# Two recurrence units get their first four k tiles in the opening, and one attention unit moves between the pairs

## The chip, the cores and the metric

The kernel runs on one core of one Trainium2 chip. The metric is the device time of one execution in microseconds. Before the change three runs took 2498.23 to 2498.86 us, median 2498.66.

## The reference, cut to what matters

A stream x of 256 tokens and 2048 features goes through two layers, each a mixer and a SwiGLU feed-forward network. Every sublayer starts with an RMS norm and a modulation by a vector c (shift, scale and gate are products of silu(c) with a large matrix, mod_w). The first mixer is the one that the change touches:

```python
def hgrn2_fox_mixer(h, w_in, w_out, lower_bound, a_out_gain, q_gain, k_gain, f_bias):
    proj = h @ w_in
    qa, fa, ia, ga, qb, kb, vb, gb, fb = jnp.split(proj, cuts, axis=-1)
    ...
    forget = lb + (1 - lb) * sig
    o_a = chunk_gated_linear_recurrence(jax.nn.silu(split_heads(qa, A_HEADS)), key,
                                        split_heads(ia, A_HEADS), log_forget)
    o_a = merge_heads(rms_norm(o_a, ...)) * jax.nn.silu(ga)
    q = rms_norm(split_heads(qb, B_HEADS), q_gain)
    ...
    o_b = forgetting_attention(q, k, split_heads(vb, B_HEADS), log_f)
    o_b = merge_heads(o_b) * jax.nn.sigmoid(gb)
    return jnp.concatenate([o_a, o_b], axis=-1) @ w_out
```

Eight recurrence heads (HGRN2) and eight attention heads (FoX), all 128 wide, share one input projection.

## The kernel before, in words

**Units.** Two heads make a unit: A0 to A3 for the recurrence, B0 to B3 for attention. A unit needs two products of 512 output columns: for A the half 0 gives forget gate and value, half 1 query and output gate; for B half 0 gives query and key, half 1 value and gate. A20 is half 0 of A2, and so on.

**Products.** k runs over 16 tiles of 128 features. Weights are float32 and are split into a rounded part hi (a cast on ScalarE, L167) and the rest lo (a subtraction on VectorE, L169); each k tile and each half of the tokens takes three matmuls, hi with hi, lo with hi, hi with lo (L190 to L192, 128x512). One piece is two k tiles: 12 matmuls. Raw weights come in tiles of 1 MiB (four k tiles of 512 columns), through three buffers "raw"; hi and lo have four buffers each. A product's sum lies in PSUM, 128x2x512, two buffers "pp" (tag "acc" in the trace).

**The opening** (start(), up to about 148 us) is written out by hand: on every engine the order is the program's. Weights of A00, A01, A10 and A11 lie together in start_w, 1 MiB for each k tile. For every k tile SyncE (SP) fetches two 1 MiB rows of mod_w (mod_s, L984) and one tile of start_w (raw_s, L989); VectorE sums the two mod rows with silu(c) (mod_sum, L109), which gives shift and scale for the 128 features; ScalarE forms the modulated operand (tm_s, L1015, hT_s, L1016); TensorE multiplies it with the four column groups, each with two token halves: 24 split matmuls for a group of four (L1031 to L1033: 4 x 2 x 3), or in six "plain" steps (k tiles 0, 3, 6, 9, 12, 15) eight float32 matmuls without a split (L1026; the trace counts 16 instructions). Mod rows alternate between two buffers "modraw" and the pool "h" (eight buffers). SP issues in program order, and a transfer that waits for its buffer holds up everything behind it. Within the first tile, x is normed and transposed on TensorE in four blocks.

**After the opening** the pieces follow a list: A20, A21, A30, A31, then B00 to B31, then the output projection O0. A scheduler sets the order of instructions on each engine, from the order in which drive() writes them. Ahead of each piece drive() takes steps from a list of jobs, by due time: each job has a number of ticks (pieces) in which to be done (table TICKS): the recurrence of a unit (hgrn: qkT, exponents L459, exp L460, decay products L487, scores L515, state picks L548, output L555 to L558, norm L650), the attention's probabilities and outputs, and the forget line of all attention heads (fox_gates). When half 0 of a unit ends, the job of the unit two before is finished by force. At the end of a B half 1 the value is copied out of PSUM and the gate g_B is formed in four steps, the last reader of that PSUM buffer being L794 on VectorE. Rows of mod_w for later sublayers are summed along the way.

In the tags "qk", "kd", "dec" and "st" a job's tiles have one or two buffers, so a unit's tiles wait for an older unit's.

## Time and profile before

| | |
|---|---|
| median of three runs | 2498.66 us |
| profiled execution, its own time | 2495.23 us |
| its span | 2493.5 us |
| TensorE busy, VectorE busy, ScalarE busy | 2442.0, 1772.8, 1168.8 us |
| granted TensorE clock, mean | 0.997 |
| opening: last plain matmul group ends | 147.5 us |
| A20 begins, B00 begins, O0 begins | about 148.7, 267, 496 us |

The profile is of one execution. "PE" is TensorE, "DVE" VectorE, "ACT" ScalarE, "SPq" SyncE's queue. A row of a group of instructions gives line, engine, operation, what it writes and reads, how many, busy time, mean duration in ns, and after the bar the idle time of the engine just before them with what ended it. TensorE's matmuls overlap: the duration of one is longer than the distance of two starts.

### The profile page before, as it was taken

How to read it: one execution, taken by the hardware profiler on the slowest of the kernel's cores; microseconds unless marked ns; L12 is line 12 of the kernel's file. 1: busy time of each engine (PE TensorE's matmuls, PEld its weight loads, DVE VectorE, ACT ScalarE, POOL GpSimd, SP SyncE). 2: the span in 40 equal slices, each digit the busy share in tenths (PEclk: the TensorE clock that was granted, in tenths of full speed). 3: DMA queues.
4: the chain of work that ended last, by engine and by line, in shares of the span. 5: the costliest groups of instructions: out<-in, count | busy, mean ns of one | idle time of the engine just before them, and what ended most of it. 6: DMA issues, size and time to landing. Idle time of an engine off the chain costs nothing.

```text
span 2493.5 us, 28661 instructions
## 1 busy us (share of the span) xinstructions
PE 2442.0 (98%) x11204; PEld 2002.5 (80%) x11204; DVE 1772.8 (71%) x2039; ACT 1168.8 (47%) x1625; POOL 89.6 (4%) x176
## 2 busy tenths in 40 slices
PE   7899999999999999999999999999999999999999
PEld 4578887887888888888888888888888888888887
DVE  6967887887788767767767787876776554644555
ACT  4255555545434444344345666654544344344343
POOL 0000000000000000000000000000000000000000
PEclk9999999999999999999999999999999999999999
DMA  9964767985798877777786667677486555555554
GB/s 390 420 258 168 286 253 290 347 320 215 288 367 339 318 285 285 289 286 283 286 292 208 236 246 248 250 280 260 175 313 237 188 195 189 188 191 193 190 189 148
DMA packets 93849, 647.48 MB, mean 260 GB/s; under 512 B 10417, under 2 KB 10993, under 8 KB 16401
## 3 DMA queue, kind: packets, MB, share of 16 engines
q1 hardware_dynamic: 70290, 476.59, 52.4%
q0 software_dynamic: 23424, 169.07, 18.2%
q8 instruction: 87, 1.43, 0.2%
q14 instruction: 48, 0.39, 0.0%
HBM read 641.39 MB, written 4.23 MB: 259 GB/s over the span
## 4 chain that ended last, share of the span: by engine, by line
PE 93%; DVE 4%; DMA 2%; ACT 1%; issue 1%; SPq 0%; ACTq 0%
PE acc_F L192 13%; PE acc_F L190 13%; PE acc_F L191 13%; PE acc_G L190 6%; PE acc_G L192 6%; PE acc_G L191 6%; PE acc_C L192 4%; PE acc_C L190 4%; PE acc_C L191 4%; PE acc_B L190 2%; PE acc_B L192 2%; PE acc_B L191 2%; PE acc_O L190 2%; PE acc_O L192 2%; PE acc_O L191 2%; DMA raw_s<-in_start_w_dram 2%
## 5 line engine op out<-in xcount | busy, mean ns | idle before, releaser
L169 DVE TENSOR_TENSOR lo<-raw_F,hi 128x1024 fp32r<-128x1024 f32 x352 | 429.5, 1223 | 302.3 <-ACT hi L167 302.1
L167 ACT CAST hi<-raw_F 128x1024 fp32r<-128x1024 f32 x352 | 370.6, 1054 | 478.1 <-PE acc_F L192 433.2
L192 PE MATMUL acc_F<-hi,hT_f 128*128 128x512 f32 x1408 | 551.1, 391 | 1.4 <-DVE hT_f L357 1.4
L190 PE MATMUL acc_F<-hi,hT_f 128*128 128x512 f32 x1408 | 548.7, 390 | 1.8 <-ACT hT_f L356 1.8
L191 PE MATMUL acc_F<-lo,hT_f 128*128 128x512 f32 x1408 | 548.4, 390 | 0.0
L109 DVE SCALAR_TENSOR_TENSOR mod<-mod,silu_c 128x2048 f32<-128x2048 f32 x160 | 365.3, 2284 | 4.2 <-DMA mod<-in_mod_w_dram 4.2
L169 DVE TENSOR_TENSOR lo<-raw_G,hi 128x1024 fp32r<-128x1024 f32 x176 | 214.2, 1222 | 139.3 <-ACT hi L167 139.1
L167 ACT CAST hi<-raw_G 128x1024 fp32r<-128x1024 f32 x176 | 185.4, 1055 | 268.5 <-PE acc_G L192 227.3
L192 PEld LDWEIGHTS acc_F<-hi,hT_f 128*128 128x128 f32 x1408 | 264.4, 188 | 56.9 <-DVE hT_f L357 3.0
L190 PEld LDWEIGHTS acc_F<-hi,hT_f 128*128 128x128 f32 x1408 | 264.5, 188 | 55.8 <-ACT hT_f L356 2.2
L191 PEld LDWEIGHTS acc_F<-lo,hT_f 128*128 128x128 f32 x1408 | 264.3, 188 | 55.1
L190 PE MATMUL acc_G<-hi,ct_f 128*128 128x512 f32 x704 | 273.5, 389 | 1.6 <-DVE res_G L405 1.6
L192 PE MATMUL acc_G<-hi,ct_f 128*128 128x512 f32 x704 | 274.4, 390 | 0.0
L191 PE MATMUL acc_G<-lo,ct_f 128*128 128x512 f32 x704 | 273.7, 389 | 0.0
L190 PEld LDWEIGHTS acc_G<-hi,ct_f 128*128 128x128 f32 x704 | 132.2, 188 | 29.6 <-DVE res_G L405 2.4
L191 PEld LDWEIGHTS acc_G<-lo,ct_f 128*128 128x128 f32 x704 | 132.2, 188 | 27.4
L192 PEld LDWEIGHTS acc_G<-hi,ct_f 128*128 128x128 f32 x704 | 132.2, 188 | 27.2
L190 PE MATMUL acc_C<-hi,hT_n 128*128 128x512 f32 x384 | 152.4, 399 | 0.9 <-ACT hT_n L356 0.9
L192 PE MATMUL acc_C<-hi,hT_n 128*128 128x512 f32 x384 | 151.3, 394 | 0.7 <-DVE hT_n L357 0.7
L191 PE MATMUL acc_C<-lo,hT_n 128*128 128x512 f32 x384 | 151.7, 395 | 0.0
L104 POOL DMA_DIRECT2D mod<-in_mod_w_dram x160 | 84.5, 528 | 1612.8 <-DVE mod L109 1449.8
L169 DVE TENSOR_TENSOR lo<-raw_C,hi 128x1024 fp32r<-128x1024 f32 x96 | 116.1, 1220 | 35.2 <-ACT hi L167 34.8
(343 smaller groups left out, 3399.7 us busy)
## 6 DMA issues: line engine op xcount, KB each, us to landing
raw_F<-in_ffn_w_in_dram SPq DMA_DIRECT2D x176, 1024.0 KB, 4.9
mod<-in_mod_w_dram POOLq DMA_DIRECT2D x160, 1024.0 KB, 5.2
raw_G<-in_ffn_w_out_dram SPq DMA_DIRECT2D x88, 1024.0 KB, 4.9
raw_C<-in_gla_w_in_dram SPq DMA_DIRECT2D x48, 1024.0 KB, 5.6
mod_s<-in_mod_w_dram SPq DMA_DIRECT2D x32, 1024.0 KB, 17.0
raw_B<-in_ab_w_in_dram SPq DMA_DIRECT2D x32, 1024.0 KB, 6.6
raw_s<-in_start_w_dram SPq DMA_DIRECT2D x16, 1024.0 KB, 13.9
raw_A<-in_ab_w_in_dram SPq DMA_DIRECT2D x16, 1024.0 KB, 5.0
```

The lines of the kernel that those rows point to most:

```text
L104: nc.gpsimd.dma_start(out=tile, in_=a["mod_w"][l, part * KT + j])
L109: nc.vector.scalar_tensor_tensor(tile, tile, 1.0, silu_c, ALU.mult, ALU.mult, accum_out=modc[l, part][:, j:j + 1])
L167: nc.scalar.copy(out=hi, in_=w)
L169: env["lo"] = nc.vector.tensor_tensor(lo, w, hi, ALU.subtract)
L190: nc.tensor.matmul(o, a_hi, w_hi, start=(kt == 0), stop=False)
L191: nc.tensor.matmul(o, a_hi, w_lo, start=False, stop=False)
L192: nc.tensor.matmul(o, a_lo, w_hi, start=False, stop=(kt == last))
```

## The change

Four more steps, e0 to e3, come first in the opening. They multiply k tiles 0 to 3 with the four column groups of A2 and A3 (a new array early_w, 1 MiB for each k tile). Their sums are copied from PSUM into two tiles of the pool "h" by eight copies on ScalarE, and PSUM is then used for A0 and A1's steps s0 to s15. A20, A21, A30 and A31 later begin at k tile 4 (piece 2 of 8), and an addition on VectorE brings in the stored sum when a product ends. The plain steps are now e0, s5, s8, s11 and s15. Of the mod rows part 0 always goes to "modraw" and part 1 to "h". Weights, sums and operand of the second step move to between two blocks of the transposition of x. The table for silu is loaded after step e3's copies. The units are ordered A0, A1, B0, A2, A3, B1, B2, B3, TICKS of the first two recurrences go from 12 and 19 to 8 and 16, and the unit whose job is finished by force is the one two before in the new order.

Line numbers after the change are larger by 3 (up to the middle of the program) to 36.

SP's queue in the opening, from the mod rows of tile 2 on; mod_s_k are mod rows of k tile k, raw_s the weights of A0 and A1. Before:

```order
L984 DMA mod_s_2_267<-in_mod_w_dram 128x2048
L984 DMA mod_s_2_269<-in_mod_w_dram 128x2048
L984 DMA mod_s_3_271<-in_mod_w_dram 128x2048
L984 DMA mod_s_3_273<-in_mod_w_dram 128x2048
L989 DMA raw_s_275<-in_start_w_dram 128x2048
L984 DMA mod_s_4_317<-in_mod_w_dram 128x2048
L984 DMA mod_s_4_319<-in_mod_w_dram 128x2048
L989 DMA raw_s_321<-in_start_w_dram 128x2048
L984 DMA mod_s_5_363<-in_mod_w_dram 128x2048
L984 DMA mod_s_5_365<-in_mod_w_dram 128x2048
```

After (raw_se are the early weights, raw_ss those of A0 and A1):

```order
L987 DMA mod_s_3_271<-in_mod_w_dram 128x2048
L987 DMA mod_s_3_273<-in_mod_w_dram 128x2048
L993 DMA raw_se_275<-in_early_w_dram 128x2048
L993 DMA raw_se_317<-in_early_w_dram 128x2048
L993 DMA raw_ss_359<-in_start_w_dram 128x2048
L993 DMA raw_ss_409<-in_start_w_dram 128x2048
L993 DMA raw_ss_444<-in_start_w_dram 128x2048
L987 DMA mod_s_4_478<-in_mod_w_dram 128x2048
L987 DMA mod_s_4_480<-in_mod_w_dram 128x2048
L993 DMA raw_ss_482<-in_start_w_dram 128x2048
L987 DMA mod_s_5_516<-in_mod_w_dram 128x2048
L987 DMA mod_s_5_518<-in_mod_w_dram 128x2048
```

Five weight tiles now stand in a row ahead of the mod rows of k tile 4.

ScalarE in the opening after the change, from the end of e3's operand to the first cast of s1 (hi_s from raw_se and raw_ss are the casts of weights; "waits" names the engine or queue whose signal is waited for):

```order
L170 CAST hi_s_0_361<-raw_se_317 128x1024 [waits DMAHW1_49,PE_49]
L170 CAST hi_s_1_365<-raw_se_317 128x1024 [waits PE_49]
L1137 COPY early_393<-acc_e_129 128x512 [waits PE_49]
L1137 COPY early_393<-acc_e_129 128x512
L1137 COPY early_394<-acc_e_130 128x512 [waits PE_49]
L1137 COPY early_394<-acc_e_130 128x512
L1137 COPY early_393<-acc_e_0_263 128x512 [waits PE_49]
L1137 COPY early_393<-acc_e_1_264 128x512 [waits PE_49]
L1137 COPY early_394<-acc_e_0_265 128x512 [waits PE_49]
L1137 COPY early_394<-acc_e_1_266 128x512 [waits PE_49]
L1124 ACT_TABLE_LOAD
L170 CAST hi_s_0_412<-raw_ss_359 128x1024 [waits DMAHW2_49,DVE_49]
```

The casts of s0 stand behind the eight copies and the table load.

TensorE after the change, at the end of B01 (its last matmul is the first row): the second head of unit A0 begins. ex are the exponents' matmuls, sc the scores.

```order
L195 MATMUL acc_B_1498<-hi_1742,hT_s_848 128x512
L462 MATMUL ex_A_0_0_0_1295<-lvl,lf_A_1037 128x512 [waits DVE_49,PE_49,Activation_49]
L462 MATMUL ex_A_0_0_0_1295<-lvl,lf_A_1037 128x512
L462 MATMUL ex_A_0_0_1_1299<-lvl,lf_A_1037 128x512 [waits DVE_49]
L462 MATMUL ex_A_0_0_1_1299<-lvl,lf_A_1037 128x512
L462 MATMUL ex_A_1_0_0_1304<-lvl,lf_A_1037 128x512 [waits Activation_49]
```

The head goes on from there to the first matmul of A20 (the last row below; cx is the carry, po the output):

```order
L518 MATMUL sc_A_1370<-dec_A_1_0_1303,qkTs_A_0_1273 128x64
L525 MATMUL cx_A_1377<-dec_A_1_0_1303,kd_A_0_0_1312 128x128
L528 MATMUL cx_A_1377<-qkTs_A_0_1273 128x128 x2
L561 MATMUL po_A_1407<-v_A_1036,st_79 128x128
L558 MATMUL po_A_1407<-v_A_1036,cs_A_1262 128x128
L559 MATMUL po_A_1407<-v_A_1036,st_79 128x128
L561 MATMUL po_A_1407<-v_A_1036,st_80 128x128 [waits DVE_49,Activation_49]
L558 MATMUL po_A_1407<-v_A_1036,cs_A_1381 128x128
L559 MATMUL po_A_1407<-v_A_1036,st_80 128x128
L193 MATMUL acc_A_1887<-hi_1796,hT_s_534 128x512 [waits DVE_49,PE_49]
```

No weight matmul stands between B01's last and A20's first; in the program before, the products A20 to A31 ran with these heads between their matmuls.

The diff, cut to what the change does (a line of "..." marks what is left out):

```diff
--- before.py
+++ after.py
@@ -22,14 +22,16 @@
-PLAIN = (0, 3, 6, 9, 12, 15)
+EARLY = 4
+PLAIN = (("e", 0), ("s", 5), ("s", 8), ("s", 11), ("s", 15))
+ORDER_AB = (("A", 0), ("A", 1), ("B", 0), ("A", 2), ("A", 3), ("B", 1), ("B", 2), ("B", 3))
-TICKS = dict(hgrn0=12, hgrn1=19, hgrn=14, fox_gates=6, fox_probs=6, fox_out=6,
+TICKS = dict(hgrn0=8, hgrn1=16, hgrn=14, fox_gates=6, fox_probs=6, fox_out=6,
              gla_low=3, gla_gates=4, gla_scores=15, gla_out=9, gla_turn=6)
@@ -139,10 +141,11 @@
-    def add(name, w, act, done, before=None, rate=0.0, first=False, last=False):
+    def add(name, w, act, done, before=None, rate=0.0, first=False, last=False, begin=0):
         p = Product(name, w, act, done, before, rate)
-        pieces.extend((p, k) for k in range(2 * len(w)))
+        p.begin = begin
+        pieces.extend((p, k) for k in range(begin, 2 * len(w)))
...
-                nc.tensor.matmul(o, a_hi, w_hi, start=(kt == 0), stop=False)
+                nc.tensor.matmul(o, a_hi, w_hi, start=(kt == 2 * p.begin), stop=False)
...
         def fetch_columns(kt):
             for part in (1, 0):
-                if (2 * kt + 1 - part) % 3 == 2:
+                if part == 0:
                     tl = rawp.tile([P, D], F32, tag="modraw", name=f"mod_s{part}_{kt}", bufs=2)
                 else:
                     tl = hpool.tile([P, D], F32, tag="h", name=f"mod_s{part}_{kt}")
                 nc.sync.dma_start(out=tl, in_=a["mod_w"][0, part * KT + kt])
                 raw_m[part, kt] = tl
 
-        def fetch_weights(kt):
-            raw_w[kt] = rawp.tile([P, 2048], F32, tag="raw", name=f"raw_s{kt}")
-            nc.sync.dma_start(out=raw_w[kt], in_=a["start_w"][kt])
+        def fetch_weights(i):
+            g, kt = steps[i]
+            raw_w[i] = rawp.tile([P, 2048], F32, tag="raw", name=f"raw_s{g}_{kt}")
+            nc.sync.dma_start(out=raw_w[i], in_=a["start_w" if g == "s" else "early_w"][kt])
 
...
-        def weights(kt):
-            if kt in PLAIN:
+        steps = [("e", kt) for kt in range(EARLY)] + [("s", kt) for kt in range(KT)]
+        new = [kt if g == "e" or kt >= EARLY else None for g, kt in steps]
+
+        def weights(i):
+            if steps[i] in PLAIN:
                 return None
-            return [split_weights(raw_w[kt][:, n * 1024:(n + 1) * 1024], f"s{kt}_{n}") for n in range(2)]
+            return [split_weights(raw_w[i][:, n * 1024:(n + 1) * 1024], f"s{i}_{n}") for n in range(2)]
...
-        def products(kt, ws, ns):
-
+        def products(i, ws, ns):
+
+            g, kt = steps[i]
+            end = EARLY - 1 if g == "e" else KT - 1
             for n in ns:
                 sl = slice((n % 2) * 512, (n % 2 + 1) * 512)
                 for t in range(2):
                     o = acc[n][t]
                     if ws is None:
-                        nc.tensor.matmul(o, tms[kt][:, t * P:(t + 1) * P], raw_w[kt][:, n * 512:(n + 1) * 512],
-                                         start=(kt == 0), stop=(kt == KT - 1))
+                        nc.tensor.matmul(o, tms[kt][:, t * P:(t + 1) * P], raw_w[i][:, n * 512:(n + 1) * 512],
+                                         start=(kt == 0), stop=(kt == end))
                         continue
                     hi, lo = ws[n // 2]
                     a_hi, a_lo = act(kt, t)
                     nc.tensor.matmul(o, a_hi, hi[:, sl], start=(kt == 0), stop=False)
                     nc.tensor.matmul(o, a_hi, lo[:, sl], start=False, stop=False)
-                    nc.tensor.matmul(o, a_lo, hi[:, sl], start=False, stop=(kt == KT - 1))
+                    nc.tensor.matmul(o, a_lo, hi[:, sl], start=False, stop=(kt == end))
+
+        def wide(g):
+            for u in range(2):
+                big = acc["qg", u] = env["pp"].tile([P, 2, 512], F32, tag="pp", name=f"acc_{g}{u}")
+                acc[2 * u + 1] = [big[:, t] for t in range(2)]
+
+        def narrow(g):
+            for u in range(2):
+                acc[2 * u] = [ps_mix(f"acc_{g}{u}_{t}") for t in range(2)]
...
         acc = {}
+        early = env["early"] = {}
         env["pp"] = ctx.enter_context(tc.tile_pool(name="pp", bufs=2, space=PSUM))
-        for u in range(2):
-            big = acc["qg", u] = env["pp"].tile([P, 2, 512], F32, tag="pp", name=f"acc_s{u}")
-            acc[2 * u + 1] = [big[:, t] for t in range(2)]
+        wide("e")
...
                 scaled(nb, 0, nc.scalar)
                 scaled(nb, 1, nc.vector)
                 turned(nb)
+                if nb == 1:
+                    fetch_weights(1)
+                    columns(1)
+                    operand(1)
+                    fetch_columns(2)
         env["pm"] = ctx.enter_context(tc.tile_pool(name="pm", bufs=4, space=PSUM))
-        for u in range(2):
-            acc[2 * u] = [ps_mix(f"acc_s{u}_{t}") for t in range(2)]
+        narrow("e")
         products(0, None, (0, 2))
-        fetch_weights(1)
-        columns(1)
-        operand(1)
-        fetch_columns(2)
-        for kt in range(1, KT):
-            if kt + 2 < KT:
-                fetch_columns(kt + 2)
-            if kt + 1 < KT:
-                fetch_weights(kt + 1)
-                columns(kt + 1)
-            if kt == 3:
+        for i in range(len(steps)):
+            if i + 2 < len(steps) and i > 0 and new[i + 2] is not None:
+                fetch_columns(new[i + 2])
+            if i + 1 < len(steps):
+                if i > 0:
+                    fetch_weights(i + 1)
+                if i > 0 and new[i + 1] is not None:
+                    columns(new[i + 1])
+            if i == 4:
                 nc.scalar.preload_act_table_set(SILU)
-            ws = weights(kt)
-            if kt + 1 < KT:
-                operand(kt + 1)
-            products(kt, ws, (1, 3, 0, 2))
+            if i > 0:
+                ws = weights(i)
+            if i > 0 and i + 1 < len(steps) and new[i + 1] is not None:
+                operand(new[i + 1])
+            if i > 0:
+                products(i, ws, (1, 3, 0, 2))
+            if i == EARLY - 1:
+                for u in range(2):
+                    early[u] = hpool.tile([P, 2, 2, 512], F32, tag="h", name=f"early_{u}")
+                for half in (1, 0):
+                    for u in range(2):
+                        for t in range(2):
+                            nc.scalar.copy(out=early[u][:, half, t], in_=acc[2 * u + half][t])
+                wide("s")
+                narrow("s")
...
         for u in range(2):
-            env["last", u] = job(hgrn_scores(u, 0) + hgrn_scores(u, 1) + hgrn_output(u), TICKS[f"hgrn{u}"])
-
+            env["last", ("A", u)] = job(hgrn_scores(u, 0) + hgrn_scores(u, 1) + hgrn_output(u), TICKS[f"hgrn{u}"])
+
+
+    def before_last(kind, u):
+
+        return ORDER_AB[ORDER_AB.index((kind, u)) - 2]
 
     def done_hgrn(u, half):
         def done(ps):
+            nc.vector.tensor_tensor(ps, ps, env["early"][u - 2][:, half], ALU.add)
             if half == 0:
-                finish(env["last", u - 2])
+                finish(env["last", before_last("A", u)])
                 urgent.extend(hgrn_gates(u, [(slice(0, 2), ps)]))
             else:
                 assert not urgent
                 env["A", u]["qg"] = hgrn_silu(u, ps)
-                env["last", u] = job(hgrn_scores(u, 0) + hgrn_scores(u, 1) + hgrn_output(u), TICKS["hgrn"])
+                env["last", ("A", u)] = job(hgrn_scores(u, 0) + hgrn_scores(u, 1) + hgrn_output(u), TICKS["hgrn"])
         return done
 
     def done_fox(u, half):
         def done(ps):
...
-                finish(env["last", u + 2])
+                finish(env["last", before_last("B", u)])
...
-                env["last", u + 4] = job(fox_output(u) + ([lambda: end_mix("out_b")] if u == 3 else []), TICKS["fox_out"])
+                env["last", ("B", u)] = job(fox_output(u) + ([lambda: end_mix("out_b")] if u == 3 else []), TICKS["fox_out"])
         return done
...
-    for u in (2, 3):
+    for kind, u in ORDER_AB[2:]:
         for half in range(2):
-            add(f"A{u}{half}", quads(a["ab_w_in"][2 * u + half]), now_act, done_hgrn(u, half), rate=RATES["A"])
-    for u in range(4):
-        for half in range(2):
+            if kind == "A":
+                add(f"A{u}{half}", quads(a["ab_w_in"][2 * u + half]), now_act, done_hgrn(u, half), rate=RATES["A"], begin=EARLY // 2)
+                continue
             before = (lambda: job(fox_gates(), TICKS["fox_gates"])) if (u, half) == (0, 0) else None
             add(f"B{u}{half}", quads(a["ab_w_in"][8 + 2 * u + half]), now_act, done_fox(u, half), before, RATES["B"])
...
+    for name, gs, n in (("start_w", groups[:4], KT), ("early_w", groups[4:8], EARLY)):
+        s = np.stack([w[:n * P, g] for g in gs])
+        arrays[name] = np.ascontiguousarray(s.reshape(4, n, P, 512).transpose(1, 2, 0, 3)).reshape(n, P, 2048)
```

More of the change, by code (lines that the diff above doesn't have):

```diff
@@ L1377, in _layout @@
     arrays["ab_w_in"] = _tiles(w, groups)
-    s = np.stack([w[:, g] for g in groups[:4]])
-    arrays["start_w"] = np.ascontiguousarray(s.reshape(4, KT, P, 512).transpose(1, 2, 0, 3)).reshape(KT, P, 2048)
+    for name, gs, n in (("start_w", groups[:4], KT), ("early_w", groups[4:8], EARLY)):
+        s = np.stack([w[:n * P, g] for g in gs])
+        arrays[name] = np.ascontiguousarray(s.reshape(4, n, P, 512).transpose(1, 2, 0, 3)).reshape(n, P, 2048)
     arrays["fb_w"] = np.ascontiguousarray(w[:, 8192:].reshape(KT, P, 8).transpose(1, 0, 2)).reshape(P, KT * 8)
```

## The prediction

> **What bounds the kernel now.** I read the page first (busy shares and the chain), then the stages as windows, then in each stage what TensorE waits for.
>
> ```profile
> span 2493.5 us, 28661 instructions
> PE 2442.0 (98%) x11204; PEld 2002.5 (80%) x11204; DVE 1772.8 (71%) x2039; ACT 1168.8 (47%) x1625; POOL 89.6 (4%) x176
> ```
>
> TensorE (PE) is busy for 98% of the span, but that is an average. The windows split it: the opening up to 148 us, then A20 to A31 (148–267), then the B products (267–496).
>
> ```profile
> 60.00:80.00 20.00, 17.72 (x65) 11.77 (x64) 18.84 (x22) 6.77 (x10) 0.00 (x0) 1.00 1.01 420
> 100.00:120.00 20.00, 17.78 (x62) 11.31 (x61) 18.38 (x25) 6.81 (x10) 0.53 (x1) 1.00 1.01 419
> 148.00:267.00 119.00, 116.88 (x607) 99.52 (x608) 85.57 (x122) 68.72 (x126) 2.12 (x4) 1.00 0.54 195
> 331.00:388.00 57.00, 57.00 (x298) 48.35 (x296) 46.92 (x59) 26.75 (x54) 4.32 (x9) 1.00 0.70 255
> ```
>
> The columns are window, length, busy PE, PEld, DVE, ACT, POOL, granted clock, DMA share and GB/s. In the opening the DMA engines are full (share 1.01, 420 GB/s) and VectorE (DVE) nearly so (18.84 of 20); PE has slack (17.7). Afterwards PE is full and the DMA has slack (0.54 to 0.70). So the change takes work from a stage that PE sets and puts work into a stage that DMA sets. What ends the opening:
>
> ```profile
> 123.98 2.00 ACT L167 CAST hi_s<-raw_s 128x1024 fp32r<-128x1024 f32 x2 [6.88 <-DMA raw_s<-in_start_w_dram]
> 132.81 2.00 ACT L167 CAST hi_s<-raw_s 128x1024 fp32r<-128x1024 f32 x2 [5.90 <-DMA raw_s<-in_start_w_dram]
> ```
> ```profile
> 140.51 7.03 PE L1026 MATMUL acc_s<-raw_s,tm_s 128*128 128x512 f32 x16
> 148.65 0.50 PE L190 MATMUL acc_A<-hi,hT_s 128*128 128x512 f32 x1 [1.11 <-ACT qg_A L1113]
> ```
>
> The last two split steps of the opening (k tiles 13 and 14) wait 6.88 and 5.90 us for their weights from DMA. Tile 14's weights are there at 132.8, the 16 plain matmuls of tile 15 begin at 140.51, and the row's 7.03 us end at 147.5: the opening ends 14.7 us after those weights.
>
> **What the change removes.** Each of A20, A21, A30 and A31 starts at its third piece, so eight pieces of 12 matmuls go, 96 in all.
>
> ```profile
> 382.36 0.39 PE L190 MATMUL acc_B<-hi,hT_s 128*128 128x512 f32 x1
> 382.59 0.39 PE L191 MATMUL acc_B<-lo,hT_s 128*128 128x512 f32 x1
> 382.82 0.39 PE L192 MATMUL acc_B<-hi,hT_s 128*128 128x512 f32 x1
> ```
>
> A matmul shows 0.39 us, but the starts are 0.227 us apart; the pitch counts. 96 x 0.227 = **−21.8 us**, in a stage that PE sets. Eight pairs of hi cast and lo subtraction go there too, which PE hid.
>
> **What the opening gains in length.** Four steps e0 to e3: 4 MiB of weights, 16 plain matmuls and 3 x 24 split ones, eight copies out of PSUM, and a new order of the transfers.
>
> ```profile
> L109 DVE SCALAR_TENSOR_TENSOR mod_s<-mod_s,silu_c 128x2048 f32<-128x2048 f32 x30 | 67.5, 2284 | 1.3 <-DMA mod_s<-in_mod_w_dram 1.3
> L1049 ACT COPY xT<-xT 128x512 f32<-128x512 f32 x6 | 3.3, 588 | 6.9 <-PE xT L1047 6.9
> L1104 ACT ACT_TABLE_LOAD x1 | 1.3, 1283 | 0.0
> L169 DVE TENSOR_TENSOR lo_s<-raw_s,hi_s 128x1024 fp32r<-128x1024 f32 x20 | 23.5, 1218 | 3.2 <-ACT hi_s L167 3.1
> ```
> ```profile
> 33.09 5.83 PE L1026 MATMUL acc_s<-raw_s,tm_s 128*128 128x512 f32 x8 [0.68 <-ACT xT L1049]
> ```
> ```profile
> 24.83 1.76 SPq L984 DMA_DIRECT2D mod_s<-in_mod_w_dram  x2
> 38.95 0.33 SPq L989 DMA_DIRECT2D raw_s<-in_start_w_dram  x1
> 39.32 0.91 SPq L984 DMA_DIRECT2D mod_s<-in_mod_w_dram  x2
> ```
> ```profile
> raw_F<-in_ffn_w_in_dram SPq DMA_DIRECT2D x176, 1024.0 KB, 4.9
> ```
>
> These rows carry the walk. One MiB at 420 GB/s takes 2.49 us in a full stream; issued into an idle queue it lands 4.9 us later (the raw_F row), so each restart leaves about 2.4 us empty. There are three weight buffers: the fourth weight fetch was issued at 38.95, when the first plain step (8 matmuls from 33.09, 5.83 us) had released its own. Before, two mod transfers (issued at 24.83) stood ahead of that wait and kept the DMA busy. After, SP's order is mod_s 2, mod_s 3, raw_se 2, raw_se 3, raw_ss 0, 1, 2 and only then mod_s 4. So while raw_se 3 waits until PE ends e0 (39.5: 38.9 plus the second tile's operand, now ahead of it), SP can issue nothing else, and the stream stands still for about 3 us. PE: e1 to e3 at 24 x 0.227 = 5.45 us each, 39.5 to 55.8. The last copies out of PSUM (0.59 each, overlapping PE's last groups) end at 57.0, the table load (1.28) at 58.3, both casts of s0 at 60.4, its second subtraction (1.22) at 61.7. raw_ss 3 waits for that buffer, and mod_s 5 behind it: issued 61.7, landed 66.6, the two mods at 71.6. From there each step needs 3 MiB, 7.48 us, more than DVE's step (two sums of 2.28 and two subtractions of 1.22, 7.0 us and some small ones). To the weights of s14 it is 1 + 10 x 3 = 31 MiB: 71.6 + 77.3 = 148.9, or 151.6 if the masks and level tables (1.07 MB, loaded by POOL in the same stretch) go ahead. Plus 14.7: PE ends at 163.6 to 166.3. I take the middle, 165, **+17.5 us** on 147.5. Bounds: +10.0 is 4 MiB without any pause (4 x 2.49); +23 is the later figure with one more restart of 2.4 and PE's stall of 4.7 before s0 (55.8 to 60.5) only half absorbed.
>
> By the Trainium skill ("DMA: Bandwidth & Descriptors", section "Where 436 GB/s comes from") a core's DMA tops out near 435 GB/s. The trace shows 419 to 420 in the full windows; by the page's figure the 31 MiB would take some 2.6 us less.
>
> **What the new order of units exposes.** B0 now comes ahead of A2, and only 16 pieces lie between the end of the opening and A20. In PE's order the second head of unit A0 stands bare between B01's last matmul and A20's first: 8 exponent matmuls, the scores, the carry and the output products, with no filler. A20's first matmul waits for DVE's g_B, which gives B01's PSUM buffer back and stands on DVE behind that head. The prices:
>
> ```profile
> L515 PE MATMUL sc_A<-dec_A,kd_A 128*128 128x64 f32 x96 | 11.7, 272 | 0.0
> L460 ACT ACTIVATE dec_A<-ex_A 128x512 f32<-128x512 f32 x17 | 9.6, 601 | 5.5 <-PE ex_A L459 5.5
> L548 DVE COPY_PREDICATED st<-lmask,sc_A 128x128 f32<-128x128 int32 x20 | 7.1, 354 | 3.7 <-ACT st L540 3.2
> L487 DVE TENSOR_TENSOR dec_A<-dec_A,qkTs_A 128x1024 f32<-128x1024 f32 x4 | 4.9, 1218 | 0.0
> L487 DVE TENSOR_TENSOR kd_A<-dec_A,qkTs_A 128x896 f32<-128x896 f32 x4 | 4.3, 1086 | 1.5 <-ACT dec_A L460 1.5
> L487 DVE TENSOR_TENSOR kd_A<-dec_A,qkTs_A 128x384 f32<-128x384 f32 x8 | 4.2, 550 | 0.0
> L650 ACT ACTIVATE oj_A<-po_A 128x128 f32<-128x128 f32 x8 | 2.2, 275 | 0.9 <-PE po_A L556 0.8
> ```
> ```profile
> L794 DVE SCALAR_TENSOR_TENSOR g_B<-acc_B,g_B 128x512 f32<-128x512 f32 x2 | 1.4, 681 | 0.0
> ```
>
> In a row: exponents 8 x 0.23 = 1.9, the last exp 0.6, the decay products on DVE about 4.1 (1.09, two of 0.55 less overlap, 1.08, 1.22), the rest of the scores after them 1.5, the state picks 5 x 0.354 and one wide 0.45 = 2.2, output products 1.5, four squares with their sums 1.9, the small rsqrt chain 1.4, g_B 0.7: 15.8 us. PE is busy in 7.4 of them (1.9, 14 score rows worth 3, carry 1, output 1.5), so **+8.5 us** idle; bounds 3 (the head's first half already runs while B01 ends) and 11 (the first head's chain is late too). At B11 to B20 and B21 to B30 the waits for g_B are of a kind that this trace shows:
>
> ```profile
> PE acc_B L190 <- DVE g_B L794: 4.3, 2, 4.1
> ```
> ```profile
> 387.62 0.39 PE L192 MATMUL acc_B<-hi,hT_s 128*128 128x512 f32 x1
> 392.08 0.55 PE L190 MATMUL acc_B<-hi,hT_s 128*128 128x512 f32 x1 [4.07 <-DVE g_B L794]
> 392.43 0.63 PE L191 MATMUL acc_B<-lo,hT_s 128*128 128x512 f32 x1
> 392.85 0.63 PE L192 MATMUL acc_B<-hi,hT_s 128*128 128x512 f32 x1
> ```
> ```profile
> 392.20:396.00 3.80, 3.80 (x10) 3.02 (x11) 1.23 (x5) 2.94 (x19) 0.00 (x0) 0.55 0.96 384
> ```
>
> After the change, ACT's list between B11's end and the g_B that B20 waits for holds three copies out of PSUM (0.6 each), three steps of g (0.6 each), a cast (1.05), eight squares with their sums (0.52 each) and three exps of the next recurrence (0.6):
>
> ```profile
> L721 ACT ACTIVATE qk_B<-acc_B 128x128 f32<-128x128 f32 x24 | 6.3, 292 | 2.9 <-PE acc_B L192 2.3 <-DVE o_A L656 0.6
> L721 ACT ACTIVATION_READ_ACCUMULATOR qk_B<-acc_B 128x1 f32 x24 | 5.4, 224 | 0.0
> L294 ACT ACTIVATE g_B<-acc_B 128x512 f32<-128x512 f32 x2 | 1.2, 605 | 0.0
> ```
>
> That is 10.6 us, some of it under the product's end, so 10.2; PE has transposes, exponents and scores for 4.3 of it, 5.9 idle. Ahead of B30 the same kinds come to 5.2 with 1.9 busy, 3.3 idle. Less the 4.3 of today: **+5 us** (bounds 0 and 8). After the 4.07 us gap today the next matmuls start 0.42 apart and the granted clock is 0.55 up to 396: nine matmuls at 0.2 more, 1.8 us. Three gaps for one, some of them broken by small matmuls: **+2** (0 to 4).
>
> The Trainium skill ("TensorE: Matmul & The Clock Gate", "HAM oscillation — how this bites in real kernels") says that a wait that crosses the clock's activity window makes the next work start cold; the trace agrees (0.55). By it every one of the gaps pays, and this last term would be near +4.
>
> **At nothing.** The four sums with the stored partials (128x1024 on DVE, taken at 1.22 each like the subtraction of that size) come where DVE has 10 of 57 us free; without that cover, 1.2 each. One more mod sum (2.28) falls into O0's end, where DVE waits before the residual; bare it would be 2.3.
>
> **Sum:** 17.5 − 21.8 + 8.5 + 5 + 2 = +11.2 us. The profiled execution (2495.23, of which the span is 2493.5) would be 2506.4. The median of the runs, 2498.66, is 3.4 above it, so the prediction is **2510**.
>
> **The rivals.**
> *Faster: the recurrence keeps ahead.* If unit A0's second head ends before B01's last matmul and the g_B of B11 and B21 find filler, no bare chain stays, and today's 4.3 and 1.8 go too: 17.5 − 21.8 − 6.1 = −10.4, **2488**. It decides once the gaps together are under some 3 us. For it: PE had 57.00 of 57.00 us in 331–388, so such heads can hide. Against it: PE's order is fixed, and it puts the head behind the product. Chance 0.2.
> *No change: the transfers don't pause.* Weights and mods queue early enough, the opening grows by 10.0, and the chains cost as above: 10 − 21.8 + 15.5 = +3.7, **2502**. For it: transfers are issued 14 us and more ahead of their landing. Against it: the fourth weight fetch already waits for its buffer in this trace (38.95). With half-covered chains and the full 17.5 the sum is also near zero. Chance 0.18.
> *Worse: DVE sets B0.* 16 pieces of B0 take 48 us of PE, and two recurrences' heads with the mods' sums fill DVE about as long; with a late first head (+11), +8, +4 and an opening of +21, +22, **2521**. Within the 0.62 for slower, about 0.12.
>
> **How the numbers follow.** About 0.2% (5 us) is what a measurement of this kernel can tell from no change. Forecast and worse case together 0.62 slower, 0.18 same, 0.20 faster. The range 2489 to 2521 leaves out the end of the faster rival and what lies past the worse one. The forecast's own range, with its terms at half their bounds, is 2503 to 2517.
>
> **What would show it.** In the changed profile: the opening's last matmul near 165 (the walk is right) or near 157 (no pause); DMA windows of 30 to 70 us under 1.0; the wait of A20's first matmul for g_B, with PE idle some 8 us around it; waits for g_B at B20 and B30 of 5.9 and 3.3. The prediction fails if the opening ends ahead of 159, or if these three gaps together are under 6 us.

## The result: 26 us slower, where 11 were forecast

The changed kernel takes 2524.61 us (median of 4 runs), the kernel before 2498.44 on the same chip: a ratio of 1.0110, 95% interval 1.0098 to 1.0122. The direction was right; the forecast of 2510 and its range (2489 to 2521) were too low. Medians here and below are of fast runs: one slow execution of `fetch_ahead_old_order` (5313.86 us) and one of `early_attention_copies` (6386.27 us) are left out. First the page of the changed kernel:

```profile
span 2523.0 us, 28699 instructions
PE 2458.2 (97%) x11212; PEld 2017.5 (80%) x11212; DVE 1779.6 (71%) x2045; ACT 1176.7 (47%) x1635; POOL 90.0 (4%) x176
```

The change took 96 matmuls of A2 and A3 away and put 88 instructions for them into the opening, yet PE is busy for 16 us more than before (2458.2 for 2442.0). (The opening has 104 matmul instructions more: two of its steps for A0 and A1 that were plain are now split, 24 instructions for 16.) The stretch of the A and B units and that of the output projection O0 as windows, first of the kernel before:

```profile
148.60:496.20 347.60, 340.44 (x1745) 288.69 (x1746) 279.13 (x383) 195.98 (x415) 20.69 (x40) 1.00 0.71 262
496.20:601.10 104.90, 101.79 (x497) 84.78 (x495) 80.20 (x101) 51.06 (x79) 5.28 (x10) 1.00 0.79 303
```

and of the changed kernel, with the end of its opening ahead of them (the last plain step, and the first matmul of B00):

```profile
163.93 7.03 PE L1036 MATMUL acc_s<-raw_ss,tm_s 128*128 128x512 f32 x16
...
172.07 0.50 PE L193 MATMUL acc_B<-hi,hT_s 128*128 128x512 f32 x1 [1.11 <-ACT qg_A L1144]
```
```profile
172.00:523.40 351.40, 331.61 (x1649) 280.35 (x1650) 272.19 (x376) 187.29 (x408) 20.24 (x39) 0.95 0.65 243
523.40:630.70 107.30, 103.10 (x497) 85.73 (x495) 82.19 (x102) 50.84 (x79) 5.83 (x11) 0.98 0.83 309
```

| stretch | before | after | difference |
|---|---|---|---|
| opening, to the end of its last matmul | 147.5 | 171.0 | +23.4 |
| A and B units, from their first matmul to that of O0 | 347.6 | 351.4 | +3.8 |
| O0, to the first matmul of the feed-forward network | 104.9 | 107.3 | +2.4 |
| the rest | 1892.4 | 1892.3 | 0 |

The two profiled spans differ by 29.5 us, the medians by 26.2: the profiled execution of the kernel before lay 3.2 under its median, that of the changed kernel (2524.72) on it. The second row is the one to read. PE's busy time there fell by 8.8 us where 21.8 us of work went, at a granted clock of 0.95 for 1.00, and its idle time (length less busy) rose from 7.2 to 19.8.

What stands in the opening, on SP's queue and on the scalar engine:

```profile
38.14 0.33 SPq L993 DMA_DIRECT2D raw_se<-in_early_w_dram  x1
40.25 8.14 SPq L993 DMA_DIRECT2D raw_ss<-in_start_w_dram  x3
48.44 1.13 SPq L987 DMA_DIRECT2D mod_s<-in_mod_w_dram  x2
61.97 0.33 SPq L993 DMA_DIRECT2D raw_ss<-in_start_w_dram  x1
```
```profile
57.21 1.28 ACT L1124 ACT_TABLE_LOAD   x1
58.50 3.89 ACT L170 CAST hi_s<-raw_ss 128x1024 fp32r<-128x1024 f32 x4
...
154.62 1.99 ACT L170 CAST hi_s<-raw_ss 128x1024 fp32r<-128x1024 f32 x2 [5.98 <-DMA raw_ss<-in_start_w_dram]
```
```profile
40.00:50.00 10.00, 10.00 (x45) 8.24 (x44) 8.04 (x11) 4.28 (x6) 0.00 (x0) 1.00 0.85 310
50.00:60.00 10.00, 6.97 (x30) 5.38 (x29) 0.42 (x1) 7.07 (x11) 0.00 (x0) 0.94 0.75 307
60.00:70.00 10.00, 9.54 (x32) 7.41 (x32) 5.75 (x6) 4.50 (x5) 0.00 (x0) 0.72 0.69 270
```

The DMA share, 1.01 in the kernel before from 20 to 120 us, is 0.85, 0.75 and 0.69 between 40 and 70 us. In the same 50 to 60 us the vector engine works for 0.42 us.

What PE waits for behind the opening (171 to 248 us, then 345 to 525 us), a view of waits each:

```profile
PE acc_A L193 <- DVE g_B L797: 3.9, 1, 3.9
PE sc_A L518 <- DVE dec_A L490: 3.6, 1, 3.6
...
```
```profile
PE sc_A L518 <- ACT fr_B L289: 3.4, 1, 3.4
PE pT_B L784 <- ACT s_B L778: 2.8, 1, 2.8
```

### The profile page after: what moved, and what is told of

Same layout as the page of the kernel before. It is cut to its first block, busy times and chain, and to the rows that moved or that the text cites. A ratio compares the mean times of both kernels' runs of the same rounds, so it can differ in the third digit from the quotient of the medians.

```text
span 2523.0 us, 28699 instructions
## 1 busy us (share of the span) xinstructions
PE 2458.2 (97%) x11212; PEld 2017.5 (80%) x11212; DVE 1779.6 (71%) x2045; ACT 1176.7 (47%) x1635; POOL 90.0 (4%) x176
## 3 DMA queue, kind: packets, MB, share of 16 engines
q0 software_dynamic: 23424, 169.07, 18.3%
## 4 chain that ended last, share of the span: by engine, by line
PE 92%; DVE 4%; DMA 2%; ACT 1%; issue 0%; SPq 0%; ACTq 0%; DVEq 0%
PE acc_F L195 13%; PE acc_F L193 13%; PE acc_F L194 13%; PE acc_G L193 6%; PE acc_G L195 6%; PE acc_G L194 6%; PE acc_C L195 4%; PE acc_C L193 3%; PE acc_C L194 3%; PE acc_B L193 2%; PE acc_B L194 2%; PE acc_B L195 2%; PE acc_O L193 2%; PE acc_O L194 2%; PE acc_O L195 2%; DVE mod_s L111 2%
## 5 line engine op out<-in xcount | busy, mean ns | idle before, releaser
L170 ACT CAST hi<-raw_F 128x1024 fp32r<-128x1024 f32 x352 | 370.6, 1054 | 463.9 <-PE acc_F L195 420.4
```

Source lines behind the costliest of these rows:

```text
L170: nc.scalar.copy(out=hi, in_=w)
```

## The experiments

Theory after the result: the opening pays for pauses of the DMA stream besides its 4 MiB; behind it, recurrence chains stand bare because eight pieces of cover are gone, and each bare stretch costs twice, as idle time and as work at the half clock.

### One half of the change at a time

`early_only`: early sums and new opening, but the old order and ticks.

```diff
-ORDER_AB = (("A", 0), ("A", 1), ("B", 0), ("A", 2), ("A", 3), ("B", 1), ("B", 2), ("B", 3))
+ORDER_AB = (("A", 0), ("A", 1), ("A", 2), ("A", 3), ("B", 0), ("B", 1), ("B", 2), ("B", 3))
...
-TICKS = dict(hgrn0=8, hgrn1=16, hgrn=14, fox_gates=6, fox_probs=6, fox_out=6,
+TICKS = dict(hgrn0=12, hgrn1=19, hgrn=14, fox_gates=6, fox_probs=6, fox_out=6,
```

> The early partial sums and the changed opening stay; the order of units and the ticks are those of before. Theory (the opening costs about 23 us, the new order of units costs the rest): the opening ends near 171 us as in the changed kernel, the products of A and B lose their 21.8 us with no bare chains, so the time is 2498 to 2504 us. Rival (the early sums themselves, through the additions and the held buffers, cost the time behind the opening): 2515 to 2524 us.

`order_only`: the kernel before with the new order, ticks and finishing rule, all 32 pieces of A2 and A3, no early sums.

> The opening of before, all 32 pieces of A2 and A3, but the units in the new order with its ticks and its rule of what is finished by force. Theory (bare recurrence chains between the units, idle and at the half clock): 2515 to 2524 us, with the wait for g_B at A20 and matmuls at the half clock around it. Rival (the order costs nothing by itself, the early sums do): 2497 to 2503 us.

| | old order | new order |
|---|---|---|
| no early sums | 2498.1 | 2508.9 (ratio 1.0042, 1.0027 to 1.0057) |
| early sums | 2533.6 (1.0143, 1.0128 to 1.0158) | 2524.6 |

Neither time that I expected held, nor either rival's range. The new order by itself costs 10.8 us, half of what I had put on it; the early sums and their opening by themselves cost 35.5, and the new order takes 9 of these back.

In `order_only` the stretch of the A and B units takes 361.5 us for 347.6, although all 32 pieces are there. Unit A0's second head, with the end of the first, stands bare ahead of A20 as it does in the changed kernel: 24.5 us without a weight matmul, at a granted clock of 0.68, with these waits in it:

```profile
199.00:223.50 24.50, 16.96 (x93) 15.29 (x91) 13.38 (x28) 9.09 (x28) 0.53 (x1) 0.68 0.28 104
```
```profile
PE acc_A L191 <- DVE g_B L795: 3.9, 1, 3.9
PE sc_A L516 <- DVE dec_A L488: 2.8, 1, 2.8
```

So the new order makes this gap, as the prediction said.

In `early_only` the opening ends at 169.3, and the stretch of the A and B units takes 347.1 us, as long as before in spite of the eight missing pieces. O0, to the feed-forward network, takes 119.4 for 104.9. The waits of the units (170 to 518 us), the largest of O0 (517 to 640 us), and what the scalar engine waits for there:

```profile
PE acc_B L193 <- DVE g_B L797: 11.4, 2, 7.5
PE sc_A L518 <- DVE dec_A L490: 3.0, 2, 1.9
```
```profile
PE pT_B L784 <- ACT s_B L778: 9.0, 1, 9.0
```
```profile
566.11 1.99 ACT L170 CAST hi<-raw_O 128x1024 fp32r<-128x1024 f32 x2 [7.25 <-DMA raw_O<-in_ab_w_out_dram]
```

The gap in O0 comes with late weights: the scalar engine's casts, which stand ahead of s_B, wait 7.25 us for them. Why they are late was not tested. In the units a likely reason, not tested by itself, is that the recurrences of A0 to A3 have 24 pieces of A2 and A3 beside them in place of 32, and are finished by force that much sooner. The additions of the stored sums are not the cause: in both kernels with early sums on A2 and A3 the four take 1.23 us each, and what waits for them waits 0.2 us in all. Each half thus makes gaps of its own, at different places, and in the changed kernel the costs overlap: 26 us, where the two halves add up to 46.

### Is it the DMA order that lengthens the opening?

`fetch_ahead`: the same bytes and arithmetic; mod rows of k tiles 4 and 5 are fetched between the early weights and summed ahead of s0, later ones by a table of steps.

```diff
+        sum_at = {1: [2], 2: [3], 3: [4], 4: [5], 6: [6], 7: [7], 9: [8], ... 17: [14], 18: [15]}
+        fetch_at = {1: [3], 2: [4], 3: [5], 4: [6], 5: [7], 7: [8], ... 15: [14], 16: [15]}
```

> The changed kernel, only the opening reordered: the mod rows of k tiles 4 and 5 are fetched between the early weights and summed before the first step of A0 and A1, later ones run ahead of their use by less and less. Same bytes, same arithmetic. Theory (the opening is lengthened by pauses of the DMA stream on top of the 10 us of volume): DMA full from 10 to 145 us, the opening ends at 157 to 161 instead of 171, the time is 2511 to 2516 us. Rival (vector engine or volume set the end, the pauses are covered): 2522 to 2526 us.

`fetch_ahead_old_order`: the same with the old order and ticks.

> The reordered opening and the old order of units together. Theory (both costs are separate and add up): 2486 to 2491 us, faster than the kernel before. Rival (pauses covered): 2498 to 2504 us. Rival (the early sums cost behind the opening): above 2505 us.

`fetch_ahead`: 2518.99 us (1.0083, 1.0068 to 1.0098), 5.6 under the changed kernel. Its opening:

```profile
50.00:60.00 10.00, 7.31 (x33) 5.72 (x31) 8.89 (x10) 5.29 (x11) 0.00 (x0) 0.99 1.01 416
60.00:70.00 10.00, 6.58 (x21) 4.98 (x22) 8.28 (x12) 6.17 (x8) 0.00 (x0) 0.67 1.01 419
```
```profile
155.56 7.03 PE L1036 MATMUL acc_s<-raw_ss,tm_s 128*128 128x512 f32 x16
```

The DMA is full between 50 and 70 us, and the opening ends at 162.6 for 171.0: the pauses that this order takes away cost 8.4 us, short of the 10 to 14 I expected, and the run missed its 2511 to 2516. `fetch_ahead_old_order` took 2525.89 (1.0108, 1.0088 to 1.0128), far above my 2486 to 2491: the second rival, that the early sums cost behind the opening, held. Its stretches behind the opening (347.7 and 119.5 us) are those of `early_only`; the opening's gain was there too (it ends at 162.3 for 169.3, the run is 7.7 us shorter).

`fetch_ahead2`: mod rows of two steps go ahead of weight fetches that wait for a plain step, the sums of tile 5 behind the first split.

> The reordered opening with two more repairs: mod rows go ahead of the two weight fetches that wait for a plain step to end (3.5 and 3.9 us of DMA pause seen in the first reordered opening), and the sums of k tile 5 go behind the first split of A0 and A1. Order of units as changed. Theory: the opening ends at 155 to 159 us instead of 162.6, the time is 2511 to 2516. Rival (by now TensorE's own work sets the opening): 161 to 163 us and no change from 2519.

2518.12 us (1.0078, 1.0063 to 1.0093), the opening at 162.9: no change, the rival held. From 100 to 140 us PE is now busy without a break (20.00 of 20.00 us in both windows), so from there PE's own steps set the end, and it depends on when they begin (61.9 us).

### Is it the clock?

`warm`: 15 matmuls without a use ahead of the scores of unit A0's second head, 16 ahead of its last output products.

```diff
             b0 = ps_mix(f"sc0_A{u}{h}")
+            if (u, h) == (0, 1):
+                for _ in range(15):
+                    nc.tensor.matmul(b0, c["r"].lf[:, 0, 0, 0:P], lvl[:, 0:512], start=True, stop=True)
```

> The changed kernel with 15 matmuls without a use ahead of the scores of unit A0's second head, and 16 ahead of that head's output products: they run where TensorE stands idle between B01 and A20 (3.6 and some 4 us) and are worth 3.4 and 3.6 us of work. Theory (the idle gap lets the clock fall, and the work behind it runs at half rate): the 28 score instructions behind the gap take 3.1 us instead of 6.1, the stretch from B01 to A20 shortens by 2 to 4 us, the run by as much. Rival (the slow scores wait for operands, the clock is not the cause): the scores stay at 6.1, the stretch grows by up to 7 us.

PE between B01 and A20 in the changed kernel:

```profile
232.73 2.70 PE L518 MATMUL sc_A<-dec_A,kd_A 128*128 128x64 f32 x12 [3.56 <-DVE dec_A L490]
235.23 0.63 PE L518 MATMUL sc_A<-dec_A,qkTs_A 128*128 128x64 f32 x2
235.65 2.76 PE L518 MATMUL sc_A<-dec_A,kd_A 128*128 128x64 f32 x12
...
247.97 0.76 PE L193 MATMUL acc_A<-hi,hT_s 128*128 128x512 f32 x1 [3.89 <-DVE g_B L797]
```

and with the filling:

```profile
228.61 3.70 PE L624 MATMUL sc_A<-lvl,lf_A 128*128 128x512 f32 x15
232.24 1.55 PE L518 MATMUL sc_A<-dec_A,kd_A 128*128 128x64 f32 x12
233.64 0.39 PE L518 MATMUL sc_A<-dec_A,qkTs_A 128*128 128x64 f32 x2
233.86 1.50 PE L518 MATMUL sc_A<-dec_A,kd_A 128*128 128x64 f32 x12
```

The same instructions take 1.55 us for 2.70 (all 28 score instructions 3.4 for 6.1), and they begin as soon after B01's last weight matmul as before (5.3 us for 5.4), although 3.7 us of useless work stands ahead of them. The granted clock of the stretch is 0.93 for 0.63 (227.3 to 248 us):

```profile
227.30:248.00 20.70, 12.33 (x55) 11.09 (x54) 9.72 (x21) 7.64 (x24) 0.00 (x0) 0.63 0.14 54
```
```profile
227.30:248.00 20.70, 16.91 (x91) 14.08 (x90) 10.26 (x22) 9.58 (x39) 0.00 (x0) 0.93 0.15 52
```

The stretch without a weight matmul shrank from 20.7 to 18.3 us (226.9 to 245.2), as expected; that the gap causes the slow work behind it is shown for this stretch. That the run gains as much is not: 2523.28 is 1.3 under the changed kernel's median, less than the runs' scatter.

### Where the cover is taken from

If cover is what was lost, the early tiles belong on units beside which no recurrence runs. `early_attention`: the reordered opening, early tiles on B1 and B2, old order and ticks, all 32 pieces of A2 and A3.

```diff
-                add(f"A{u}{half}", quads(a["ab_w_in"][2 * u + half]), now_act, done_hgrn(u, half), rate=RATES["A"], begin=EARLY // 2)
+                add(f"A{u}{half}", quads(a["ab_w_in"][2 * u + half]), now_act, done_hgrn(u, half), rate=RATES["A"])
...
-            add(f"B{u}{half}", quads(a["ab_w_in"][8 + 2 * u + half]), now_act, done_fox(u, half), before, RATES["B"])
+            add(f"B{u}{half}", quads(a["ab_w_in"][8 + 2 * u + half]), now_act, done_fox(u, half), before, RATES["B"], begin=EARLY // 2 if u in (1, 2) else 0)
...
-    for name, gs, n in (("start_w", groups[:4], KT), ("early_w", groups[4:8], EARLY)):
+    for name, gs, n in (("start_w", groups[:4], KT), ("early_w", groups[10:14], EARLY)):
```

> The same opening, but the four early k tiles belong to the attention units B1 and B2 instead of A2 and A3, in the old order of units with the old ticks: the 32 pieces that cover the first recurrences stay, eight pieces go from the attention units. Theory (what was lost behind the opening is the cover of the recurrence): A20 to the output projection takes 326 to 332 us instead of 347.6, the run 2486 to 2494 us, faster than the kernel before. Rival (any eight pieces cover something, the gaps come back elsewhere): 2500 to 2515 us.

2508.88 us (1.0041, 1.0026 to 1.0056). The time is in the rival's range. The A and B units take 329.0 us, 18.6 less than in the kernel before: this part of the theory held, though 13.8 us between B11 and B20 are now without a weight matmul (4.1 before). But O0 to the feed-forward network takes 120.4 for 104.9. In that stretch (494 to 615 us) PE waits longest at the feed-forward network's start:

```profile
PE acc_F L193 <- ACT hT_f L359: 5.9, 1, 5.9
PE acc_O L193 <- DVE res_O L408: 2.0, 1, 2.0
```

Beside every B piece a share of the mod rows is summed. Eight pieces fewer are about four sums fewer (half of 1.05 for each piece), and these now stand in O0: it has 14 for 10, four of them in its last 25 us, where the kernel before has none. They do not explain all of it: a second gap of 10.0 us without a weight matmul (4.2 before) stands in the middle of O0.

`early_attention_rate`: `RATES` A = 0.6 for 0.3, to sum them beside the A pieces.

> The early tiles on B1 and B2 as before, one number changed: the rate at which mod rows are summed beside the A pieces, 0.6 for 0.3. Theory (the eight missing B pieces took 4 of these sums with them, which then stand bare around the output projection, 10.0 us without a weight matmul there and 9.5 us ahead of the feed-forward network): the stretch from O0 to F0 falls from 120 us to 105 to 109, the run to 2494 to 2499 us. Rival (the output projection waits for the attention unit itself or for weights): 118 to 120 us there, 2507 to 2510 us.

2518.04 us (1.0077, 1.0063 to 1.0091), slower, and outside both ranges. O0 to the feed-forward network fell to 113.7 and has 10 sums again, with 10.8 us still bare in its middle; and the scheduler put a whole second head bare between B11 and B20: 23.3 us without a weight matmul, with these waits:

```profile
400.04 2.79 PE L518 MATMUL sc_A<-dec_A,kd_A 128*128 128x64 f32 x12 [5.55 <-DVE dec_A L490]
...
415.38 0.77 PE L193 MATMUL acc_B<-hi,hT_s 128*128 128x512 f32 x1 [3.89 <-DVE g_B L797]
```

`early_attention_copies`: the same, with s0's split and the table load ahead of the eight copies.

```diff
             if i == EARLY - 1:
+                ahead = weights(EARLY)
                 for u in range(2):
                     early[u] = hpool.tile(...)
```

> The same, and in the opening the split of the first A0/A1 tile and the table load stand ahead of the eight copies on the scalar engine. Theory (TensorE's 6 us between e3 and s0 are the copies, the load and the split in a row): s0 begins at 57 to 59 us instead of 61.9, the opening ends 2 to 4 us earlier, at 159 to 161, the run 2490 to 2497 us. Rival (the opening is set by DMA again, and the gain is taken back later): 162 to 163 us and no change.

2513.36 us (1.0059, 1.0045 to 1.0072): s0 begins at 58.2 for 61.8 and the opening ends at 157.2 for 162.8, 5.6 us, more than expected; the run is 4.7 shorter. It stays 14.4 us over the kernel before, far from the expected 2490 to 2497, and still has the rate of 0.6 and a bare head of 23.3 us.

`early_last_units`: this opening, rate 0.3 again, early tiles on B2 and B3.

> The opening with the early split ahead of the copies, the old order of units and the old ticks and rates, and the early four k tiles on B2 and B3, the last two attention units: the 32 pieces of A2 and A3 and all 16 of B1 stay as cover until the last recurrence is over. Theory (a gap opens wherever a recurrence has fewer pieces beside it than it had): no bare score-and-output stretch between B11 and B20 (it was 13.8 to 23.3 us with the early tiles on B1 and B2), the opening ends at 157 to 158, A20 to the output projection takes 326 to 332 us, the run 2489 to 2499 us, so equal to or faster than the kernel before. Rival (any eight pieces take cover from something): 2500 to 2510.

2501.49 us (1.0014, 1.0005 to 1.0023), in the rival's range. The bare head between B11 and B20 is gone; the wait for g_B there is 4.1 us, as in the kernel before:

```profile
PE acc_B L193 <- DVE g_B L797: 5.9, 3, 4.1
```

Its A and B units take 323.2 us, less than expected. But O0 takes 124.3 us to the feed-forward network, with the missing sums again: 14 for 10, four of them at its end. (The profiled execution shows a mean clock of 0.943, which the others did not; the last section says what that did.)

`last_units_sums` (rate 1.4 beside B1 and B2) and `last_unit_sums` (1.4 beside B3, 0.9 beside O0):

> The early tiles on B2 and B3 as in the run before this one, and one number changed: mod rows are summed at a rate of 1.4 for 1.05 beside the pieces of B1 and B2, so that none is left for the end of the output projection. Theory (the 19 us that O0 to F0 lost, 124.3 for 104.9, are the sums that went with the eight pieces): 105 to 113 us there, the run 2489 to 2496 us, faster than the kernel before by 2 to 9 us. Rival (the sums press on the vector engine where they go instead, and the gap moves into B): 2499 to 2506 us.

> The same with the rates set elsewhere: 1.4 beside the pieces of B3 alone and 0.9 for 0.8 beside the output projection; one sum is left for its end. Theory: 106 to 116 us from O0 to F0, the run 2490 to 2498 us. Rival (the last unit is bound by the vector engine): 2499 to 2506 us.

2500.78 (1.0014, 1.0005 to 1.0023) and 2500.48 us (1.0008, 0.9999 to 1.0017). The rival held in both. In the first, O0 to the feed-forward network is down to 114.0 and the stretch of A and B up to 334.9. In the second they are 114.6 and 332.3, and a gap sits at the end of B3:

```profile
PE pT_B L784 <- ACT s_B L778: 5.7, 1, 5.7
```

The best of these equals the kernel before within what can be told. With the opening down to 157.6, about the 4 MiB alone, the change trades about 10 us there for up to 22 in the pieces, and each place from which the eight pieces were taken gave most of it back. Whether an arrangement exists that keeps a gain isn't shown; none of those tried did.

## Why the prediction was wrong, step by step

**The eight pieces, −21.8:** the work went as worked out (96 matmuls fewer in the window). What came in its place was priced too low, in the clock and in the opening.

**The opening, +17.5 forecast, +23.4 measured.** The walk was right to the middle: SP's fetch of raw_ss 3 was forecast for 61.7 and came at 61.97, and the mod rows behind it landed at 71.9 for 71.6. From there the step "31 MiB in a full stream" failed: the cast of s14 began at 154.6, not between 148.9 and 151.6. That is 4.4 us on the middle that I chose. The masks took their place in the stream (1.3 of it); further short pauses (share 0.95 to 0.99 from 70 to 100 us) come to about as much, and the rest was not followed. The last 1.6 us are the 16.3 us from that cast to the end, for 14.7 before, at a clock of 0.86 between 140 and 160 us. So in the prediction's terms 13.4 us came on top of the bare 4 MiB, where 7.5 were forecast. That the pauses are real, and that 8.4 us go when the fetches, and with them the sums, are reordered, `fetch_ahead` shows; the growth of 10.0 in my "no change" rival was reached only after the copies were moved as well (157.2).

**The bare chains, +8.5 and +5:** right in sum. PE's idle time from the first matmul behind the opening to the feed-forward network rose by 13.7 us (12.6 among the units, 1.1 in O0). Between B01 and A20 it is 3.56, 0.92 and 3.89, 8.4 us for 8.5, and `order_only` shows that the order makes this gap. For the rest the sum is in part luck, since the places differ: 5.3 at B11 to B20 for 5.9, but in waits other than the one for g_B that I named; none at B21 to B30 for 3.3; some 3 us each at the end of A21 and in B2, which I had not named.

**The clock, +2 (0 to 4): the step that failed.** I counted nine slow matmuls behind a gap, as after the 4.07 us gap of the kernel before. There the gap was followed by dense weight matmuls, and the clock came back within 4 us. A bare chain is different: its short instructions stand between further waits, and the clock stayed low for most of 20 us. The windows give the size. In the two stretches behind the opening PE was busy for 434.7 us; the 442.2 of before less 21.8 would be 420.4. The same instructions thus took **+14.3** us longer in place of +2, at mean clocks of 0.95 and 0.98 for 1.00. That the clock is the cause of all of it was not shown; it was in the stretch that `warm` filled, where the clock and the durations went back together. With the 13.7 us of idle time that is more than the 21.8 saved.

The Trainium skill ("TensorE: Matmul & The Clock Gate", "HAM oscillation — how this bites in real kernels") describes such a repeated fall of the clock as a cost of waits between bursts. I had drawn +4 from it, one full price for each gap. The traces agree with the rule (0.63 in the bare stretch, 0.93 with the gaps filled) and show the price to hang on what follows the gap.

**Nothing for the sums (2.3 if bare), and O0:** O0 has the one sum more (11 for 10) and takes 2.4 us more, of which 1.1 are idle time, with a wait of 1.9 for the last attention unit's output; the mechanism was not followed further. The four additions cost PE nothing that the trace shows.

In sum: 23.4 − 21.8 + 13.7 + 14.3 = 29.6 us, the 29.5 of the profiled spans. The terms behind the opening are read from the same windows as the whole, so this is a division of the difference and not a second proof of it. The forecast of 11.2 was too low by 12.3 in the clock and 5.9 in the opening. Against the medians (26.2) the profiles show 3.3 us more, because the profiled execution of the kernel before was a quick one.

Two small sums of the prediction are off, neither of which decides anything: 15.8 less 7.4 is 8.4, and the terms at half their bounds add up to 2500 to 2517, not 2503.

The rivals: "faster" fell, since the gaps it needed covered are there. "No change" had the opening's pauses wrong. "Worse" (2521) had the size nearly, but its mechanism, the vector engine setting B0, was not seen: B00 and B01 took 55 us with PE busy throughout. My theory after the result, that the new order costs all that the opening does not, fell in the two half changes: the order costs 10.8 alone, and with the early sums it saves.

## What to carry to other kernels

Work taken from a stage that is bound by one engine also takes the cover from everything scheduled beside it: before moving it, list what runs in those pieces (dependent chains, sums at a rate for each piece) and where each goes. Price a bare dependent chain as idle time and, for its own matmuls, at the low clock. And when transfers are added to a full DMA stream, read the issue queue's order for the first fetch that waits for a buffer: what stands behind it stops too.

## What was not expected of the hardware

The clock's price came to more than half of the waits that caused it: in the stretch between B01 and A20 PE idled 8.4 us, and work that was priced at 7.4 us by the rows of the kernel before took 12.3. Useless matmuls in the waits raised the clock from 0.63 to 0.93 and made the chain 2.4 us shorter. And one execution of `early_last_units` shows a clock near 0.95 through its whole span, at 2504.72 us for a median of 2501.49. In dense work this lower figure cost nothing: the first row is of that execution, the second of `last_unit_sums`, both in the feed-forward network, with the same number of matmuls.

```profile
700.00:1200.00 500.00, 500.00 (x2239) 414.10 (x2238) 379.02 (x346) 208.04 (x215) 29.16 (x55) 0.95 0.83 309
700.00:1200.00 500.00, 500.00 (x2239) 414.47 (x2238) 378.26 (x346) 206.81 (x214) 28.51 (x54) 1.00 0.83 307
```
